# Where the rows of the MLP's operands start in SBUF: multiples of 128 bytes, or steps of 16 bytes and places off a 16-byte line

## The chip, the core and the metric

The kernel runs on one core of a Trainium2 chip. The metric is the device time of one execution in microseconds (us). The time before is the median of three runs. One further execution was recorded by the hardware profiler; the rows that are shown below come from it.

The engines are called as in the profile: PE is TensorE's matrix multiplication, PEld its loading of weights, DVE is VectorE, ACT is ScalarE, POOL is GpSimd and SP is SyncE, which here only issues DMAs. SBUF is the memory on the chip. It has 128 partitions, and a tile lies at the same byte address in all of them, so "where a row starts" is one number.

## The reference

A decoder block on 16 learned tokens and 256 input tokens, with a model width of 2048. A mixer of two attention branches comes first, then a squared-ReLU MLP of width 8192, then a norm. All of it is float32.

```python
for l in range(DEPTH):      # DEPTH = 1
    h = h + hybrid_mixer(rmsnorm(h, norm_mix_g[l]), w_in[l], ...)
    h = h + squared_relu_mlp(rmsnorm(h, norm_mlp_g[l]), w_ff1[l], w_ff2[l])
return rmsnorm(h, final_norm_g)[:, N_META:]

def squared_relu_mlp(xn, w1, w2):
    return jnp.square(jax.nn.relu(xn @ w1)) @ w2
```

`w1` is 2048 x 8192 and `w2` is 8192 x 2048.

## The kernel before

Everything is held transposed: 128 channels lie on the partitions, tokens along the row. 2048 channels are 16 blocks, called k.

Each float32 factor is cut in two, a high part in the type float32r and the remainder, and a product is made of the terms that matter. An operand tile has one row for each k. The row has 2 x 256 columns, the high parts of the 256 tokens and then the low parts. `mac2` (lines 135 to 137) makes two matmuls for each k: a wide one, the high part of the weights (`whi`) on all 512 columns, and a narrow one, the low part (`wlo`) on the first 256. `gemm2` runs them over 16 k into one PSUM bank, so one product of 128 output channels is 32 matmuls. The weights of the next matmul are loaded into TensorE while the present one streams its columns.

Weights come in chunks of 128 x 2048 in the order of `stream()`. SyncE issues two DMAs of 512 KB for each chunk into `raw` (five buffers). ScalarE casts `raw` to `whi` (line 120), and VectorE subtracts to get `wlo` (line 121). Both have five buffers of 4096 bytes a partition, with one k every 512 bytes.

The order of the instructions is worked out by a planner, which simulates the program on a timeline; it may move instructions of one product a little among those of the next.

The MLP runs in four quarters (`for g in range(NG)`, lines 885 to 903). A quarter makes 16 products of `x2` with the first matrix (line 889), and `relu2` turns each into one row of `a` (total, maximum and norm, square, and `split_to`, lines 877 to 882). Then it makes 16 products of `a` with the second matrix, which are added to the residual `h` (line 898). `x2` is written before, a row at a time, as the mixer's last products end (lines 864 to 867). In the last quarter the last four products are made in another order: the low weights on the high part (L912), and then the kept high weights `whi_last` on half of the tokens at a time, 2 x 128 columns (L928).

Operand tiles come from the helper `operand()` (line 218). `og` and `x2` stand one after the other in the slot "s2", which `whi_last` takes over at the end; `x`, `y` and the four `a` stand in the slot "s1". `of` stands in the pool "late". In all of them a row is 2 x 256 columns with 32 columns left out behind it, so rows are 544 columns, 2176 bytes, apart, and the first starts 16 columns, 64 bytes, from the tile's place (for `of` 48 columns from it):

```python
row = 2 * NT + 32
t = pool.tile([P, at + nk * row], F32R, name=nm(name), **kw)
t = t[:, at:].rearrange("p (k r) -> p k r", r=row)
return t[:, :, 16 : 16 + 2 * NT].rearrange("p k (o t) -> p k o t", t=NT)
```

In the allocation of this program, every `whi` and `wlo` buffer starts at 128 modulo 512 bytes, the slots s1 and s2 start at 64, and `whi_last`, which begins with its slot, starts at 64 too.

Of the kernel before, what the change touches and what calls it, by code (L numbers as in the profile page):

```python
# [8 lines left out]
F32R = mybir.dt.float32r  # L9
# [7 lines left out]
P = 128  # L17
D = 2048
KT = D // P
NM = 16  # L20
NT = 256
NA = NM + NT
EPS = 1e-6
FOX_H, FOX_D = 8, 128
# [41 lines left out]
def trunk(ctx: ExitStack, tc: tile.TileContext, hT, w_small, w_all, consts, w_alpha2, out):  # L66
# [3 lines left out]
    def nm(s):  # L70
        serial[0] += 1
        return f"{s}_{serial[0]}"

    const = ctx.enter_context(tc.tile_pool(name="const", bufs=1))
    keep = ctx.enter_context(tc.tile_pool(name="keep", bufs=1))
# [49 lines left out]
    def next_weights(keep_hi=None):  # L125
        c = chunk[0]
        chunk[0] += 1
        parts = []
        for i in range(2):
            hi, lo, step = weight_half(c, i, None if keep_hi is None else keep_hi[:, HK * i : HK * (i + 1), :])  # L130
            step(0, HK)
            parts.append((hi, lo))
        return lambda k: (parts[k // HK][0][:, k % HK, :], parts[k // HK][1][:, k % HK, :])
# [5 lines left out]
    def gemm2(w, x, k0=0, nk=KT):  # L139

        ps = bank(pg, "ps")
        for k in range(nk):
            hi, lo = w(k0 + k)
            mac2(ps, hi, lo, x[:, k], k == 0, k == nk - 1)
        issued()
        return ps
# [18 lines left out]
    def total(ps, t=None):  # L165

        b = tmp.tile([P, NT], F32, tag="evb", name=nm("evb"))
        nc.scalar.copy(b, ps[:, NT:512])  # L168
        if t is None:
            t = tmp.tile([P, NT], F32, tag="evt", name=nm("evt"), bufs=4)  # L170
        nc.vector.tensor_tensor(t, ps[:, 0:NT], b, op=ALU.add)  # L171
        return t
# [42 lines left out]
            nc.vector.scalar_tensor_tensor(r, r, -0.5, v, op0=ALU.mult, op1=ALU.mult)  # L215
            nc.vector.scalar_tensor_tensor(y, r, 1.5, y, op0=ALU.add, op1=ALU.mult)

    def operand(pool, name, nk=KT, at=0, **kw):


        row = 2 * NT + 32
        t = pool.tile([P, at + nk * row], F32R, name=nm(name), **kw)
        t = t[:, at:].rearrange("p (k r) -> p k r", r=row)
        return t[:, :, 16 : 16 + 2 * NT].rearrange("p k (o t) -> p k o t", t=NT)


    h = keep.tile([P, KT, NA + 3], F32, name="h")
# [26 lines left out]
    def gain(i, k):  # L254
        return h[:, k, NA + i : NA + i + 1]
# [60 lines left out]
    for s in range(KT // 2):  # L316
# [5 lines left out]
        for kk in range(2):  # L322
            k = 2 * s + kk
# [15 lines left out]
        at = [(w[0][:, c], w[1][:, c]) for w, n in ((wa, 4), (wb, 3)) for c in range(n)]  # L339
# [118 lines left out]
    def og_tile():  # L458
        if not og_box:
            og_box.append(operand(keep, "og", tag="s2"))  # L460
        return og_box[0]
# [220 lines left out]
    cum.close()  # L682
    branches = ExitStack()
    late = branches.enter_context(tc.tile_pool(name="late", bufs=1, reuse_waits="tile"))
    of = operand(late, "of", FOX_H, 32)
    negc = late.tile([P, FOX_H, NA], F32, name="negc")
    nc.gpsimd.dma_start(negc.rearrange("p h t -> p (h t)"), fdram.to_broadcast([P, FOX_H * NA]))
    fox = ExitStack()
# [137 lines left out]
    for j0 in range(0, KT, 2):  # L826
        gates = ahead if j0 == 0 else [gate() for _ in range(4)]
        w = next_weights()
        for j in range(2):
            t = total(gemm2(w, of, k0=8 * j, nk=8))  # L830
            nc.vector.tensor_tensor(gates[2 * j], gates[2 * j], t, op=ALU.mult)
        for j in range(2):
            t = total(gemm2(next_weights(), og))
            nc.vector.tensor_tensor(t, gates[2 * j + 1], t, op=ALU.mult)
            nc.vector.tensor_tensor(yf[:, j0 + j, :], gates[2 * j], t, op=ALU.add)
    y = operand(keep, "y", tag="s1")
    for j in range(KT):
        split_to(y[:, j, 0, :], y[:, j, 1, :], yf[:, j, :])
# [4 lines left out]


    ht = h[:, :, NM:NA]
    x2 = operand(keep, "x2", tag="s2")

    def square_sum(j, acc):
        if j == 0:
            nc.scalar.activation(acc, ht[:, j, :], AF.Square)  # L850
        else:
            sq = gat.tile([P, NT], F32, tag="hsq", name=nm("hsq"))
            nc.scalar.activation(sq, ht[:, j, :], AF.Square)  # L853
            nc.gpsimd.tensor_tensor(acc, acc, sq, op=ALU.add)  # L854

    def add_residual(j, ps):
        b = tmp.tile([P, NT], F32, tag="evb", name=nm("evb"))
        nc.scalar.copy(b, ps[:, NT:512])
        nc.vector.tensor_tensor(ht[:, j, :], ps[:, 0:NT], ht[:, j, :], op=ALU.add)
        nc.vector.tensor_tensor(ht[:, j, :], ht[:, j, :], b, op=ALU.add)  # L860
# [16 lines left out]
    def relu2(a, f, ps):  # L877
        t = total(ps)
        nc.vector.scalar_tensor_tensor(t, t, 0.0, r2b, op0=ALU.max, op1=ALU.mult)
        s = gat.tile([P, NT], F32, tag="asq", name=nm("asq"))  # L880
        nc.vector.tensor_tensor(s, t, t, op=ALU.mult)
        split_to(a[:, f, 0, :], a[:, f, 1, :], s)

    acc = gat.tile([P, NT], F32, tag="acc", name="acc3", bufs=1)
    for g in range(NG):
        a = operand(keep, "a", tag="s1")
        held = []
        for f in range(KT):
            ps = gemm2(next_weights(), x2)
            if g == 0 and f == 0:  # L890
                held.append(ps)
                continue
            if g == 0 and f == 1:
                relu2(a, 0, held.pop())
            relu2(a, f, ps)
        last = g == NG - 1
        for j in range(KT - NL if last else KT):
            add_residual(j, gemm2(next_weights(), a))
            if last:
                square_sum(j, acc)  # L900
                nc.scalar.activation(ht[:, j, :], ht[:, j, :], AF.Identity, scale=gain(2, j))
                if j == 0:
                    tc.keep_in_program_order(nc.scalar.preload_act_table_set("natural_log_exp_and_others"))
# [155 lines left out]
```

## Time and profile before

| | us |
|---|---|
| median of 3 runs | 1597.07 (1596.95 to 1597.44) |
| span of the profiled execution | 1595.0 |
| PE busy in it | 1585.0 |
| DVE busy | 1060.4 |
| ACT busy | 790.8 |

The profiled execution's own time is its span of 1595.0 us and 2.07 us less than the median of the runs.

How to read the profile's rows. A group of instructions has its line, engine and operation, the tile that is written and those that are read, the shape, the count, then the busy time in us and the mean in ns of one, then the idle time of its engine before it. The duration of a matmul runs on through the pipeline after the last column is in, so matmuls in a stream overlap: the time from one start to the next is less than the duration. Differences between durations of one form can be compared. In the chain in order of time a piece has its start, its length, and how many instructions it merges. Slices are fortieths of the span, in tenths.

### The profile page before, as it was taken

What the parts mean: (1) busy time and instruction counts of PE and PEld (TensorE: products, weight loads), DVE (VectorE), ACT (ScalarE), POOL (GpSimd) and SP (SyncE); (2) the same over time, 40 slices, a digit from 0 to 9 for tenths busy, and PEclk for the clock granted to TensorE, in tenths of its full rate; (3) what the DMA queues carried; (4) which work ended last, traced back from release to release, by engine and by line L of the source; (5) the groups of instructions that cost most, each with busy time, mean ns of one, the idle gap of its engine ahead of it and who ended that gap; (6) DMA issues with size and microseconds to landing.
All of it is one profiled execution on the core that took longest, in us unless ns stands there. A gap on an engine that the chain in (4) does not pass through costs nothing.

```text
span 1595.0 us, 25427 instructions
## 1 busy us (share of the span) xinstructions
PE 1585.0 (99%) x9812; PEld 1428.8 (90%) x9812; DVE 1060.4 (66%) x1659; ACT 790.8 (50%) x1271; POOL 125.2 (8%) x213
## 2 busy tenths in 40 slices
PE   9999999999999999999999999999999999999997
PEld 8999999999998888888888888888888888888887
DVE  7897757676655555555777776567655776567655
ACT  6665444454455444444555544444444444444563
POOL 6011000011100000000011000000000000000022
PEclk9999999999999999999999999999999999999999
DMA  9444545454445555555555555555555555555552
GB/s 323 156 164 155 180 157 183 167 188 164 159 167 181 191 186 189 189 191 187 186 195 186 188 193 187 188 191 190 187 190 190 186 189 193 186 188 193 186 183 97
DMA packets 86602, 293.09 MB, mean 184 GB/s; under 512 B 9112, under 2 KB 16800, under 8 KB 86352
## 3 DMA queue, kind: packets, MB, share of 16 engines
q1 hardware_dynamic: 85872, 289.62, 53.8%
q8 instruction: 77, 1.26, 0.3%
q0 software_dynamic: 176, 1.12, 0.2%
q10 hardware_dynamic: 432, 0.72, 0.1%
q14 instruction: 45, 0.37, 0.1%
HBM read 289.32 MB, written 2.11 MB: 183 GB/s over the span
## 4 chain that ended last, share of the span: by engine, by line
PE 99%; DMA 0%; issue 0%; POOL 0%; ACT 0%; DVE 0%; SPq 0%; POOLq 0%; ACTq 0%
PE ps L136 51%; PE ps L137 27%; PE psa L155 5%; PE psa L154 5%; PE psa L153 5%; PE ps L345 1%; PE ps L350 1%; PE ps L928 1%; PE pa L548 1%; PE ps L912 0%; DMA raw<-w_all_dram 0%; PE po L611 0%; POOL o L976 0%; PE po L188 0%; PE ps L348 0%
## 5 line engine op out<-in xcount | busy, mean ns | idle before, releaser
L121 DVE TENSOR_TENSOR wlo<-raw,whi 128x1024 fp32r<-128x1024 f32 x522 | 641.0, 1228 | 452.8 <-ACT whi L120 449.4
L120 ACT CAST whi<-raw 128x1024 fp32r<-128x1024 f32 x522 | 548.1, 1050 | 660.0 <-PE ps L136 493.1
L136 PE MATMUL ps<-x,whi 128*128 128x512 f32 x1952 | 683.8, 393 | 0.0
L137 PE MATMUL ps<-x,wlo 128*128 128x256 f32 x1952 | 548.5, 281 | 0.0
L136 PEld LDWEIGHTS ps<-x,whi 128*128 128x128 f32 x1952 | 366.1, 188 | 80.4
L137 PEld LDWEIGHTS ps<-x,wlo 128*128 128x128 f32 x1952 | 368.3, 189 | 0.1
L136 PE MATMUL ps<-a,whi 128*128 128x512 f32 x960 | 334.3, 392 | 0.0
L137 PE MATMUL ps<-a,wlo 128*128 128x256 f32 x960 | 269.1, 281 | 0.0
L136 PEld LDWEIGHTS ps<-a,whi 128*128 128x128 f32 x960 | 179.8, 188 | 39.9
L137 PEld LDWEIGHTS ps<-a,wlo 128*128 128x128 f32 x960 | 181.1, 189 | 0.3
L153 PE MATMUL psa<-x,whi 128*128 128x272 f32 x624 | 181.2, 290 | 0.0
L155 PE MATMUL psa<-x,whi 128*128 128x272 f32 x624 | 181.1, 290 | 0.0
L154 PE MATMUL psa<-x,wlo 128*128 128x272 f32 x624 | 179.4, 288 | 0.0
L153 PEld LDWEIGHTS psa<-x,whi 128*128 128x128 f32 x624 | 118.1, 189 | 0.4
L154 PEld LDWEIGHTS psa<-x,wlo 128*128 128x128 f32 x624 | 117.4, 188 | 0.0
L155 PEld LDWEIGHTS psa<-x,whi 128*128 128x128 f32 x624 | 117.2, 188 | 0.0
L136 PE MATMUL ps<-og,whi 128*128 128x512 f32 x256 | 89.6, 392 | 0.0
L136 PE MATMUL ps<-y,whi 128*128 128x512 f32 x256 | 89.1, 392 | 0.0
L854 POOL TENSOR_TENSOR acc<-acc,hsq 128x256 f32<-128x256 f32 x26 | 28.5, 1097 | 769.2 <-ACT hsq L853 769.2
L137 PE MATMUL ps<-og,wlo 128*128 128x256 f32 x256 | 71.9, 281 | 0.0
L137 PE MATMUL ps<-y,wlo 128*128 128x256 f32 x256 | 71.8, 281 | 0.0
L171 DVE TENSOR_TENSOR evt<-ps,evb 128x256 f32<-128x256 f32 x158 | 65.9, 418 | 0.5 <-ACT evb L168 0.5
(301 smaller groups left out, 1437.0 us busy)
## 6 DMA issues: line engine op xcount, KB each, us to landing
raw<-w_all_dram SPq DMA_DIRECT2D x537, 512.0 KB, 3.6
raw<-w_all_dram SPq DMA_DIRECT2D x8, 384.0 KB, 6.6
h<-hT_dram SPq DMA_DIRECT2D x8, 275.0 KB, 6.7
negc<-fdram POOLq DMA_DIRECT2D x1, 1088.0 KB, 8.0
out_dram<-o SPq DMA_DIRECT2D x2, 512.0 KB, 2.7
raw<-w_all_dram SPq DMA_DIRECT2D x2, 256.0 KB, 3.9
room<-w_small_dram SPq DMA_DIRECT2D x1, 320.0 KB, 7.4
out_dram<-o ACTq DMA_DIRECT2D x1, 320.0 KB, 3.1
```

Of the source, the lines that this page charges most:

```text
L120: nc.scalar.copy(hi[:, k, :], r)
L121: nc.vector.tensor_tensor(lo[:, k, :], r, hi[:, k, :].bitcast(F32), op=ALU.subtract)
L136: nc.tensor.matmul(ps, hi, x, start=first, stop=False)
L137: nc.tensor.matmul(ps[:, 0:NT], lo, x[:, 0, :], start=False, stop=last)
L153: nc.tensor.matmul(ps[:, 0:NA], hi, x_hi[:, k], start=(k == 0), stop=False)
L154: nc.tensor.matmul(ps[:, 0:NA], lo, x_hi[:, k], start=False, stop=(k == KT - 1))
L155: nc.tensor.matmul(ps[:, X_LO], hi, x_lo[:, k], start=False, stop=(k == KT - 1), skip_group_check=True)
L171: nc.vector.tensor_tensor(t, ps[:, 0:NT], b, op=ALU.add)
L345: nc.tensor.matmul(ps, hi, x[:, k], start=st, stop=False)
L350: nc.tensor.matmul(ps[:, 0:NT], lo, x[:, k, 0], start=False, stop=sp)
L548: nc.tensor.matmul(dst, k[:, a], q[:, a, :], start=(a == 0), stop=(a == 1))
L854: nc.gpsimd.tensor_tensor(acc, acc, sq, op=ALU.add)
```

## The change

`operand()` gets the place of the first row (`at`, in columns of 4 bytes) and the distance between rows (`row`) as arguments. With the defaults the rows stand as before, at 16 columns and 544 apart; a tile is now never larger than its rows. `of` uses the defaults, so its tile is 32 columns shorter and its first row is 16 columns from the tile's place.

`x2` has its rows from column 16, 516 columns (2064 bytes) apart. The first two `a` have theirs from column 80, also 516 apart. The third `a` starts at column 18 and the fourth at column 17, with 520 columns (2080 bytes) between rows. In bytes modulo 16 the rows of `x2` and of the first two `a` start at 0, those of the third at 8 and those of the fourth at 4. What is computed is the same, and so are the instructions and their number.

```diff
-    def operand(pool, name, nk=KT, at=0, **kw):
-
-
-        row = 2 * NT + 32
-        t = pool.tile([P, at + nk * row], F32R, name=nm(name), **kw)
-        t = t[:, at:].rearrange("p (k r) -> p k r", r=row)
-        return t[:, :, 16 : 16 + 2 * NT].rearrange("p k (o t) -> p k o t", t=NT)
+    def operand(pool, name, nk=KT, at=16, row=2 * NT + 32, **kw):
+
+        t = pool.tile([P, nk * (2 * NT + 32)], F32R, name=nm(name), **kw)
+        if at + nk * row > nk * (2 * NT + 32):
+            return t.rearrange("p (k r) -> p k r", r=row)[:, :, at : at + 2 * NT].rearrange("p k (o t) -> p k o t", t=NT)
+        t = t[:, at : at + nk * row].rearrange("p (k r) -> p k r", r=row)
+        return t[:, :, 0 : 2 * NT].rearrange("p k (o t) -> p k o t", t=NT)
...
-    of = operand(late, "of", FOX_H, 32)
+    of = operand(late, "of", FOX_H)
...
-    x2 = operand(keep, "x2", tag="s2")
+    x2 = operand(keep, "x2", at=16, row=2 * NT + 4, tag="s2")
...
-        a = operand(keep, "a", tag="s1")
+        a = operand(keep, "a", at=(80, 80, 18, 17)[g], row=2 * NT + (4, 4, 8, 8)[g], tag="s1")
```

## The prediction

> **What bounds the kernel now.** I read the page's shares, slices and chain first, then the stretch of the MLP, then the single matmuls in it.
>
> ```profile
> span 1595.0 us, 25427 instructions
> PE 1585.0 (99%) x9812; PEld 1428.8 (90%) x9812; DVE 1060.4 (66%) x1659; ACT 790.8 (50%) x1271; POOL 125.2 (8%) x213
> PEclk9999999999999999999999999999999999999999
> PE 99%; DMA 0%; issue 0%; POOL 0%; ACT 0%; DVE 0%; SPq 0%; POOLq 0%; ACTq 0%
> PE ps L136 51%; PE ps L137 27%; PE psa L155 5%; PE psa L154 5%; PE psa L153 5%; PE ps L345 1%; PE ps L350 1%; PE ps L928 1%; PE pa L548 1%; PE ps L912 0%; DMA raw<-w_all_dram 0%; PE po L611 0%; POOL o L976 0%; PE po L188 0%; PE ps L348 0%
> ```
>
> TensorE is the chain: 99% of it, at full granted clock in every slice, and 78% in the two lines of `mac2`. The executions had a median of 1597.07 us; this profiled one spans 1595.0, so 2.07 us lie around the span, and I add them to every sum.
>
> Next the MLP, cut at the borders between its halves (first matrix, second matrix, in turn). The columns are the stretch, its length, and the busy time and count of TensorE.
>
> ```profile
> 1049.76:1138.94 89.18, 89.18 (x514) 1.00 0.56 189
> 1138.94:1228.11 89.17, 89.17 (x513) 1.00 0.55 189
> 1228.11:1317.28 89.17, 89.17 (x513) 1.00 0.56 189
> 1317.28:1406.46 89.18, 89.18 (x514) 1.00 0.56 190
> ```
>
> Two stretches read `x2`, two read `a`, and all take the same 89.17 us without a gap. A half has 16 products of 16 pairs, so a wide and a narrow matmul together cost 89.17 / 256 = 0.348 us. In such a stretch nothing but the rate at which TensorE streams columns sets the time. The change touches where these columns lie, so it acts on the bound itself, with no cover over it in either direction.
>
> The matmuls by form, in the stretch that reads the third `a`:
>
> ```profile
> L136 PE MATMUL ps<-a,whi 128*128 128x512 f32 x253 | 88.1, 392 | 0.0
> L137 PE MATMUL ps<-a,wlo 128*128 128x256 f32 x252 | 70.6, 281 | 0.0
> L137 PEld LDWEIGHTS ps<-a,wlo 128*128 128x128 f32 x253 | 47.7, 189 | 0.1
> L136 PEld LDWEIGHTS ps<-a,whi 128*128 128x128 f32 x253 | 47.4, 188 | 10.5
> ```
>
> 256 more columns take 392 - 281 = 111 ns more, which is 0.434 ns a column. 16 bytes are four columns, 1.7 ns. That is my price for one more piece of 16 bytes, if TensorE fetches in such pieces.
>
> **The change part by part.** No instruction is added or taken away. What moves is the first byte of every row that a matmul streams. By the allocation of this program, each weight tile starts at 128 modulo 512 and its k steps are 512 bytes, so `whi[k]` and `wlo[k]` are always at 128. Both slots, s1 and s2, start at 64. Before, row k stands at 64 + 64 + 2176k, which is 128k from the weights' place modulo 512. After, `x2` stands at 16k, the first two `a` at 256 + 16k, the third at 8 + 32k and the last at 4 + 32k.
>
> Matmuls affected: `x2` 4 x 16 products x 32 = 2048; the first two `a` 1024; the third 512; the last 12 x 32, and 64 of L912 and 128 of L928, 576. In all 4160. The bound of 0.2%, about what a measurement of this kernel can tell from no change, is 3.2 us, or 0.77 ns for each of them. So the whole question is about fractions of a percent of a matmul.
>
> Term A, the place beside the weights. The trace shows two sets of places on the same tile `a`, both of 256 columns, in the tail where no weight is being cast: L912 against `wlo`, at multiples of 128 from the weights, and L928 against `whi_last`, whose slot starts at 64, so at odd multiples of 64.
>
> ```profile
> 1562.51 5.68 PE ps L912 x48
> ...
> 1571.96 7.47 PE ps L928 x64
> ```
>
> From the chain in order of time: 5.68 / 48 = 118.3 ns against 7.47 / 64 = 116.7 ns each. The place matters, by 1.6 ns. How much one and the same line varies as k goes through the four places it has now is in the answer for L136:
>
> ```profile
> L136 PE MATMUL ps<-a,whi x238: 388/393/397, 1317.1 to 1399.7; 128*128 128x512 f32 x119
> L136 PE MATMUL ps<-x,whi x7: 390/392/393, 1314.7 to 1316.8; 128*128 128x512 f32 x7
> ```
>
> Minimum, median and maximum: a spread of 3 to 9 ns around 392, on `x2` as on `a`. One more row shows starts that are not multiples of 64. In the GLA outputs `a0h` and its weights start 32 bytes past one, in the FoX outputs `pah` and its weights do not, with the same 256 columns:
>
> ```profile
> L190 PE MATMUL po<-a0h,v0l x16: 278/280/281, 99.3 to 302.2; 128*128 128x256 f32 x16
> L190 PE MATMUL pof<-pah,val x8: 278/278/280, 352.6 to 485.9; 128*128 128x256 f32 x8
> ```
>
> The median is 2 ns higher. So term A lies between -1.6 ns (all new places like L928's) and +2 ns (all like `a0h`'s): -6.7 to +8.3 us over 4160. A sweep in steps of 16 or 32 bytes spreads the rows evenly over half of the 512 bytes or all of them, good and bad places alike. Only a quarter of the swept places are multiples of 64, of which the rows say anything good. I take a quarter of -1.6, that is -0.4 ns: -1.7 us. [...]
>
> Term B, rows off a 16-byte line. In the last two quarters a row of 512 columns begins and ends inside a 16-byte piece, and touches 129 of them in place of 128. At 1.7 ns each for 512 + 576 = 1088 matmuls this is +1.9 us. [...] Its upper end is the rate of plain float32, the slowest streaming that the trace has:
>
> ```profile
> L548 PE MATMUL pa<-qx,kx 128*128 128x208 f32 x16 | 3.8, 359 | 0.0
> L548 PE MATMUL pa<-qx,kx 128*128 128x80 f32 x16 | 2.3, 264 | 0.0
> ```
>
> (359 - 264) / 128 = 0.742 ns a column, 0.308 above the 0.434 of the MLP's form. The last `a` is streamed over 192 x 768 + 192 x 256 = 196,608 columns, so at that rate it costs +61 us. I take +1.9: the stream is contiguous in all quarters, and only its two ends change. [...]
>
> Term C, what other engines do with the rows. ScalarE and VectorE write them, and VectorE reads one half back, at the new places:
>
> ```profile
> L121 DVE TENSOR_TENSOR wlo<-raw,whi 128x1024 fp32r<-128x1024 f32 x522 | 641.0, 1228 | 452.8 <-ACT whi L120 449.4
> L879 DVE SCALAR_TENSOR_TENSOR evt<-evt,r2b 128x256 f32<-128x256 f32 x64 | 27.0, 425 | 2.0
> L881 DVE TENSOR_TENSOR asq<-evt 128x256 f32<-128x256 f32 x64 | 27.0, 424 | 2.0
> L176 DVE TENSOR_TENSOR a<-asq,a 128x256 fp32r<-128x256 f32 x64 | 26.6, 419 | 0.0
> L171 DVE TENSOR_TENSOR evt<-ps,evb 128x256 f32<-128x256 f32 x158 | 65.9, 418 | 0.5 <-ACT evb L168 0.5
> L175 ACT CAST a<-asq 128x256 fp32r<-128x256 f32 x64 | 25.5, 401 | 0.0
> ```
>
> A product of the first matrix lasts 89.17 / 16 = 5.57 us. VectorE does 2 x 1.23 + 0.42 + 0.42 + 0.42 + 0.42 = 4.14 us in it. If the write of L176 took twice its 0.42, it would be 4.56, still under 5.57. The product that runs meanwhile hides it, so it costs 0. Without that cover the doubling would be 0.42 us for each of 64 rows, 27 us. What would be late then is the last row, `a[15]`, for the first product of the second matrix. The reuse of slots s1 and s2 adds no wait: a row is first written after a whole product on another operand, 5.57 us after the last reader of the old tile.
>
> Term D, `of`. Its tile is 128 bytes shorter, and row 0 stands 128 bytes lower. With a row step of 2176 the places are still all multiples of 128, the same set in another order of k. The tiles behind it in the late pools move by 128 bytes, and their starts modulo 64 stay. Cost 0, with at most the 2 ns of L190 on 2 calls x 3 matmuls x 8 heads, 0.1 us.
>
> The sum: 1595.0 - 1.7 + 1.9 + 2.07 = 1597.3 us.
>
> **The rivals.**
>
> Slower, by a fetch of 32 bytes. If TensorE takes rows in aligned pieces of 32 bytes, every row that does not start on one needs a further piece, 8 columns, 3.5 ns. These are half of `x2` (1024), half of the first two `a` (512) and all of the last two (1088), 2624 matmuls: +9.2 us, 1606.3. For it: no matmul of this kernel's MLP starts at an odd multiple of 16 now, so nothing excludes it. Against it: pieces of 64 bytes would cost 7 ns at `a0h`, and L190 shows 2. It decides from 1.2 ns a matmul.
>
> Much slower, by rows 4 bytes off. If a column pair that straddles a line needs two accesses, the last quarter streams near the rate of L548: +61 us, 1658. For it: the MLP's form is the fastest stream that the kernel has, so it has least to spare. Against it: nothing more than that the rows are contiguous.
>
> Faster, by better places. If multiples of 128 bytes are the worst meeting of moving rows and weights, and all other places are like L928's, the 4160 matmuls gain 1.6 ns each and the ragged ends are hidden: -6.7 us, 1590.4. For it: 118.3 against 116.7 ns. Against it: the 2 ns that `a0h` loses at a place that is no multiple of 128. It decides from 0.77 ns a matmul.
>
> The change cannot fail to take place: the rows lie where the program puts them.
>
> **How the numbers follow.** The forecast, no change that can be measured, gets 0.40, since its two terms are of one size and of opposite sign. The fetch of 32 bytes, or another cost of a few ns on ragged rows, gets 0.26, and the straddling pairs 0.11: two ways to be slower, neither excluded by any row. Better places get 0.23. So faster 0.23, same 0.40, slower 0.37. The forecast's own range is 1594 to 1600. The range of 8 in 10 reaches down to 1590, the end of term A. Upward it goes to the fetch of 32 bytes with part of term A's upper end, 1612. Left out are the straddling pairs (0.11) and some 0.06 in the tails.
>
> **What would show it.** In the profile after, each half on `x2` or on the first two `a` should take 89.17 - 512 x 0.0004 = 89.0 us, and the half on the third `a` 89.17 + 512 x 0.0013 = 89.8. If the halves on `x2` are longer than before, term A has the wrong sign. If the third and the last differ by over 1%, the bytes inside a line matter. If L136's maximum is far over 393, single rows stall. I would be wrong above all if the stream has a unit that the aligned rows of now never showed.

## The result: slower by 0.6%, nearly all of it inside the MLP

The changed kernel takes 1606.36 us (median; 1605.82 to 1606.71) against 1597.03 before (the median of four executions; 1597.07 was that of the first three). The ratio is 1.0058, with a 95% interval of 1.0046 to 1.0071. The forecast was no change that can be measured, 1597.3 us. The time lies in the range of 1590 to 1612, on the side that had 0.37, and outside the forecast's own range of 1594 to 1600.

The order of the instructions is the same on every engine. First the page of the changed kernel, its span, shares and chain by engine:

```profile
span 1605.0 us, 25427 instructions
PE 1595.2 (99%) x9812; PEld 1432.2 (89%) x9812; DVE 1059.9 (66%) x1659; ACT 790.8 (49%) x1271; POOL 124.9 (8%) x213
PE 99%; issue 0%; POOL 0%; DMA 0%; ACT 0%; POOLq 0%; DVE 0%; ACTq 0%
```

TensorE is busy 10.2 us longer, and its share of the chain is what it was. No wait has come in; the matmuls themselves are longer. The halves of the MLP, one on `x2`, one on the second `a`, one more on `x2`, the one on the third `a`, and then the twelve whole products on the fourth `a` (columns as in the prediction's windows):

```profile
1052.06:1142.19 90.13, 90.13 (x513) 1.00 0.58 187
1142.19:1232.31 90.12, 90.12 (x513) 1.00 0.59 187
1232.31:1322.44 90.13, 90.13 (x513) 1.00 0.59 187
1322.44:1413.00 90.56, 90.56 (x514) 1.00 0.58 187
1503.14:1571.55 68.41, 68.41 (x387) 1.00 0.58 186
```

Before, each half took 89.17, so twelve products took 66.88. The four halves on `x2` and the two on the first two `a`, all on 16-byte lines (a line is here no more than the 16 bytes from one multiple of 16 to the next), lose 0.96 us each, 5.8 together. The half on the third `a`, 8 bytes off a line, loses 1.39, and the twelve products on the fourth, 4 bytes off, 1.53. The tail reads the fourth `a` as well; in the chain in order of time:

```profile
1571.55 5.88 PE ps L912 x48
...
1581.32 7.84 PE ps L928 x64
```

That is 122.5 ns for each matmul of both lines, where it was 118.3 and 116.7: 64 x 4.2 + 128 x 5.8 = 1.0 us. The sum is 9.7 us. The two profiled spans differ by 10.0, of which 0.4 came ahead of the MLP (its first matmul starts at 871.42 us in place of 871.02); the medians differ by 9.3.

### The profile page after: what moved, and what is told of

Read it like the earlier page. It is cut to its first block, busy times and chain, and to the rows that moved or that the text cites. A ratio compares the mean times of both kernels' runs of the same rounds, so it can differ in the third digit from the quotient of the medians.

```text
span 1605.0 us, 25427 instructions
## 1 busy us (share of the span) xinstructions
PE 1595.2 (99%) x9812; PEld 1432.2 (89%) x9812; DVE 1059.9 (66%) x1659; ACT 790.8 (49%) x1271; POOL 124.9 (8%) x213
## 4 chain that ended last, share of the span: by engine, by line
PE 99%; issue 0%; POOL 0%; DMA 0%; ACT 0%; POOLq 0%; DVE 0%; ACTq 0%
PE ps L136 51%; PE ps L137 26%; PE psa L155 5%; PE psa L154 5%; PE psa L153 5%; PE ps L345 1%; PE ps L928 1%; PE ps L350 1%; PE pa L548 1%; PE ps L912 0%; PE po L611 0%; POOL o L976 0%; DMA h<-hT_dram 0%; PE po L188 0%; PE ps L348 0%
## 5 line engine op out<-in xcount | busy, mean ns | idle before, releaser
L136 PE MATMUL ps<-x,whi 128*128 128x512 f32 x1952 | 687.6, 395 | 0.0
L136 PEld LDWEIGHTS ps<-x,whi 128*128 128x128 f32 x1952 | 366.3, 188 | 83.9
L136 PE MATMUL ps<-a,whi 128*128 128x512 f32 x960 | 339.1, 396 | 0.0
L136 PEld LDWEIGHTS ps<-a,whi 128*128 128x128 f32 x960 | 180.6, 188 | 43.0
L136 PE MATMUL ps<-og,whi 128*128 128x512 f32 x256 | 89.5, 392 | 0.0
L136 PE MATMUL ps<-y,whi 128*128 128x512 f32 x256 | 89.1, 392 | 0.0
```

The lines of the kernel that those rows point to most:

```text
L136: nc.tensor.matmul(ps, hi, x, start=first, stop=False)
```

## Experiments

Three theories stood at the start. By the theory of the fetch in 32 bytes (a rival of the prediction, 1606.3 us) every row that does not start on a multiple of 32 costs 3.5 ns more. By the theory of the place alone, a row costs what its place relative to the weights costs, whatever stands before it. By the theory of the step, the distance between rows decides. Since all eight halves of the MLP are measured apart, one kernel can hold five layouts. Places and steps are in bytes from the weights' place, modulo 512, as in the prediction: rows 2176 bytes apart have a step of 128, rows 2048 bytes apart a step of 0. Where no ratio is given, the kernel ran once, and parts of its one trace are compared.

### Same step as before, other starts

```diff
-    x2 = operand(keep, "x2", at=16, row=2 * NT + 4, tag="s2")
+    x2 = operand(keep, "x2", at=20, row=2 * NT + 32, tag="s2")
...
-        a = operand(keep, "a", at=(80, 80, 18, 17)[g], row=2 * NT + (4, 4, 8, 8)[g], tag="s1")
+        a = operand(keep, "a", at=(24, 32, 18, 17)[g], row=2 * NT + (32, 32, 32, 32)[g], tag="s1")
```

> Rows 2176 bytes apart as before, but started off the multiples of 128: x2 at 16 + 128k from the weights' place, the four a at 32, 64, 8 and 4 + 128k. Half by half (89.17 us each before; 90.12 on x2 and on the first two a after, 90.55 on the third a after). Theory of the fetch in pieces of 32 bytes: x2 91.0, first a 89.2, second a 89.2, third a 91.0, total about +10 us. Theory of the place alone (a pair takes what the row at that place took in the trace after, period 256): x2 89.9, first a 89.5, second a 90.1, and the third and fourth more. Theory of the step (steps of 128 keep the meeting of rows and weights as it was, wherever they start): all halves on 16-byte lines within 0.2 of 89.2, and only the third and fourth a, off a line, longer, by 0.3 to 1.4.

1603.15 us. The windows of this kernel, in the order `x2` (16 off), first `a` (32), second (64), third (8):

```profile
1050.76:1140.34 89.58, 89.58 (x514) 1.00 0.58 188
961.17:1050.76 89.59, 89.59 (x515) 1.00 0.57 189
1140.34:1229.96 89.62, 89.62 (x515) 1.00 0.58 187
1319.56:1409.68 90.12, 90.12 (x515) 1.00 0.57 188
```

Rows that all start at odd multiples of 16 cost the same as rows on 32 and on 64. The fetch in 32 bytes said 91.0 against 89.2, so it falls, although the time that it gave for the change, 1606.3, is the time that was measured. The step alone does not decide either: at the same step, 0 took 89.17 and 16, 32 and 64 take 0.4 more. The row 8 bytes off costs 0.5 beyond those.

### Other steps

The lines that replace the same two of the changed kernel:

```diff
+    x2 = operand(keep, "x2", at=16, row=2 * NT + 8, tag="s2")
...
+        a = operand(keep, "a", at=(20, 16, 18, 17)[g], row=2 * NT + (8, 16, 4, 4)[g], tag="s1")
```

> Other steps: x2 at 32k from the weights' place (all even multiples of 16), first a at 16 + 32k (all odd multiples), second a at 64k, third at 8 + 16k and fourth at 4 + 16k. Theory of the fetch in pieces of 32 bytes: x2 89.2, first a 91.0, second a 89.2, third a 91.0. Theory of the place alone: x2 90.1, first a 90.1, second a 90.4. Theory of the step: x2 and first a alike, and the second a, with the larger step, nearer to 89.2 than both.

1603.94 us. `x2` on all even multiples of 16, first `a` on all odd ones, second `a` on multiples of 64, third 8 off a line at steps of 16:

```profile
1050.53:1140.33 89.80, 89.80 (x515) 1.00 0.58 188
961.12:1050.53 89.41, 89.41 (x515) 1.00 0.58 188
1140.33:1229.73 89.40, 89.40 (x515) 1.00 0.57 188
1319.54:1410.17 90.63, 90.63 (x514) 1.00 0.57 186
```

The odd multiples are the faster ones here. By the place alone, 89.41, 89.80 and 89.40 should have been 90.1, 90.1 and 90.4, so that theory falls too: one place does not have one price. By the step, `x2` and the first `a` should have been alike; they differ by 0.39.

### One place for all rows, and the weights moved instead of the rows

The same two lines again:

```diff
+    x2 = operand(keep, "x2", at=16, row=2 * NT + 0, tag="s2")
...
+        a = operand(keep, "a", at=(48, 32, 20, 64)[g], row=2 * NT + (0, 0, 0, 0)[g], tag="s1")
```

> Rows 2048 bytes apart, so that all rows of a tile stand at one place from the weights: x2 at 0, the four a at 128, 64, 16 and 192. Theory of the place alone: halves of 89.3 (x2), 92.2 (128), 88.8 (64), 89.9 (16), and the rate of the last a that of 91.4 (192). Theory of the fetch in pieces of 32 bytes: 89.2 for x2 and the first, second and fourth a, 91.0 for the third. Theory of the step: no half need follow the row of its place in the trace after; what a row costs depends on the rows before it.

The second kernel has this ahead of the weights' buffers besides:

```diff
+    gap = wp.tile([P, 16], F32, name="gap", bufs=1)
```

> As e_const, with a tile of 64 bytes put in ahead of the weights' buffers, so that the weights move by 64 bytes and the rows do not. If the place relative to the weights decides, the halves change places with e_const (period 256): the first a takes what e_const's second a took (64), the second a what e_const's x2 took (0), x2 what e_const's last a took (192), and the last a what e_const's first a took (128). If the rows' own address decides, each half is as in e_const within 0.1.

1603.37 and 1606.26 us. In the second kernel the products before the MLP meet moved weights too, so the halves are compared and not the totals. First the kernel without the gap: `x2` (0), first `a` (128), second (64), third (16):

```profile
1052.00:1142.46 90.46, 90.46 (x515) 1.00 0.58 187
962.13:1052.00 89.87, 89.87 (x515) 1.00 0.58 188
1142.46:1232.90 90.44, 90.44 (x515) 1.00 0.58 187
1321.65:1410.40 88.75, 88.75 (x514) 1.00 0.59 190
```

And with it, the same tiles in the same order, whose places are now 448, 64, 0 and 464:

```profile
1054.26:1144.69 90.43, 90.43 (x514) 1.00 0.57 186
964.83:1054.26 89.43, 89.43 (x515) 1.00 0.58 189
1144.69:1233.60 88.91, 88.91 (x514) 1.00 0.58 190
1324.04:1413.66 89.62, 89.62 (x515) 1.00 0.57 188
```

Three of the four halves shown moved though their rows did not, by 0.44 to 1.53 us. The half on `y`, ahead of the MLP, has its rows in both kernels where the kernel before has them. First without the gap, then with it:

```profile
782.61:871.78 89.17, 89.17 (x514) 1.00 0.59 191
784.70:874.32 89.62, 89.62 (x514) 1.00 0.59 190
```

Without the gap it takes 89.17 or 89.18 in every trace that leaves `y` there, the kernel before among them. With the gap its rows stand at 64 + 128k, and 89.62 is what the second `a` took at these places in the first experiment. So the rows' own address cannot be all, and where the weights stand has its part.

Of the four exchanges that the place relative to the weights foretold, the last `a`, now at 128, took the 89.87 of the first `a` there. `x2`, now at 448, took the 90.43 that the last `a` took at 192 (256 of its pairs at 353.3 ns), but it had taken 90.46 without the gap, so this one decides nothing. The two others did not come: place 0 took 90.46 in one kernel and 88.91 in the other, and place 64 took 90.44 and 89.43. Rows 2048 bytes apart at place 16 took 88.75, less than any layout so far; the fetch in 32 bytes had 91.0 for them. The prices of the theory of the place alone (89.3, 92.2, 88.8 and 89.9 in the order of the first four lines) are all missed by over 1 us.

One place has two rates even within the kernel without the gap. These are its first product on `x2`, the fourth of the same half, and the third half on `x2`:

```profile
871.78:877.33 5.55, 5.55 (x34) 1.00 0.61 190
888.64:894.29 5.65, 5.65 (x34) 1.00 0.58 190
1232.90:1321.65 88.75, 88.75 (x515) 1.00 0.59 189
```

Rows and weights stand alike in all of them. In the first half the pairs take 346 to 347 ns (5.55 us for 16) until the two matmuls of the norm (L207 and L208) come between, and from then on 349, 350 and 361 in turn (5.65 us for 16). The second and the fourth half on `x2` have the slow rate, 90.46 and 90.45; the third has the fast one. So what ran before counts, and 90.46 against 88.91 at place 0 may be these two rates, with no part in it of the moved weights.

### Blocks of pairs, measured by themselves

The kernel before, with this behind its last output; `flat` is the weights of `whi_last`, and each call is one block of pairs, whose results are not used:

```diff
+    rows = keep.tile([P, KT * 2 * NA], F32R, tag="s1", name="rows")
...
+    def block(name, place, step, shift=0, m=P, wide=True, narrow=True, wstep=P, reps=2):
...
+                row = rows[:, at + k * step // 4 : at + k * step // 4 + 512]
+                for on, c, n in ((wide, 0, 512), (narrow, 2048, 256)):
+                    if on:
+                        jobs.append((c + k * wstep + shift, row[:, 0:n], n))
+        for i, (c, r, n) in enumerate(jobs):
+            pin(nc.tensor.matmul(ps[0:m, 0:n], flat[:, c : c + m], r, start=(i == 0), stop=(i == len(jobs) - 1)))
```

> The kernel before, and behind its last output some 40 separate blocks of pairs (one wide and one narrow matmul, as in mac2) on a tile of constant rows, each block with its own place, step of rows, shift of the weights or width of the weights; so its total is some 450 us longer and only the blocks are read. Before, a pair takes 348.3 ns; on steps of 16 bytes 352.0. Theory of the meeting (rows meet the load of the next weights, and the place relative to the weights decides): moving rows and weights together by 64 or 128 bytes changes a pair by under 0.3 ns, and with weights of only 64 or 32 columns a pair gets shorter and the steps of 16 and of 128 bytes come within 1 ns of each other. Theory of the rows' own address: moving the weights alone changes nothing, and with narrow weights the difference of 3.7 ns between the two steps stays. Theory of the ragged ends (a 129th piece of 16 bytes): rows at 4, 8 and 12 bytes off a line cost the same, some 1.7 ns a matmul more than at 16, in the wide and the narrow alike. Theory of column pairs that straddle (units of 8 bytes): 8 costs what 16 does, 4 and 12 cost alike and more, and more in the wide than in the narrow.

From its chain in order of time, a block a line: start, length, name, matmuls. A block is 32 pairs. `stb` and `stf` have steps of 16 and 128 from place 0; `pla` and `plb` have rows 2048 bytes apart at places 0 and 16; `ofa` to `ofd` have steps of 128 with starts at 16, 8, 4 and 12; `ma`, `mb` and `mc` have weights of 64 columns, with steps of 128, of 16, and of 128 from 4.

```profile
1629.38 11.28 PE stb L1018 x64
...
1674.28 11.16 PE stf L1018 x64
...
1693.84 11.30 PE pla L1018 x64
1705.14 11.10 PE plb L1018 x64
...
1940.12 11.19 PE ofa L1018 x64
1951.31 11.40 PE ofb L1018 x64
1962.71 11.47 PE ofc L1018 x64
1974.17 11.10 PE ofd L1018 x64
...
2007.89 11.15 PE ma L1018 x64
2019.04 11.11 PE mb L1018 x64
2030.15 11.52 PE mc L1018 x64
```

The blocks give back what the kernels did: 11.28 / 32 = 352.5 ns a pair at steps of 16 (the halves on `x2` after: 90.13 / 256 = 352.1), 348.8 at steps of 128 (348.3 before, without the block's first matmul). So the loss needs no other engine: from 1599.58 us, the first block, to 2097.76 the chain holds matmuls alone, and no weights are cast in that time.

With weights of 64 columns the two steps come together, 11.15 and 11.11. The next kernel repeats it: 11.14 and 11.10 with 64 columns, 11.15 and 11.26 with 128. So on 16-byte lines the loss of the small step hangs on the width of the weights. Narrower weights are loaded and also make a narrower result, and the blocks do not separate the two. The pair at steps of 128 did not get shorter by it, which the theory of the meeting had wrong. The row 4 bytes off stays expensive with narrow weights (11.52), so that part, 11.52 against 11.15, is the rows' own. It is a price of each matmul and not of each column: by themselves, 32 wide matmuls took 7.36 us on a line and 7.47 at 4 off, 32 narrow ones 3.79 and 3.88, which is 3.4 and 2.8 ns for each.

Rows and weights moved together, the other test of the theory of the meeting, bear it out in part. By 64 bytes a block went from 11.16 to 11.14 and another stayed at 11.31; by 128 bytes one went from 11.10 to 11.09, but two others from 11.31 to 11.16 and from 11.30 to 11.10. So the place of the rows relative to the weights does not fix the rate by itself either.

The starts inside a line are no matter of straddling units of 8 bytes, since 8 off (`ofb`, 11.40) costs nearly what 4 off does (`ofc`, 11.47). Nor is it the 129th piece, since 12 off, which has one as well (`ofd`, 11.10), is the cheapest of the four. These are single blocks. The next kernel takes averages, and asks for the state left by the block before.

```diff
+    block("loa", 0, 2176)
+    block("lob", 16, 2176)
...
+    block("hye", 128, 2048)
+    block("hyf", 0, 2048)
```

> The kernel before with 65 blocks of pairs behind it, as in p1_blocks; only the blocks are read. What a start off a 16-byte line costs, averaged over eight places (steps of 2176 bytes from 0, 16 to 112) and not at one. Theory of the ragged ends: 4, 8 and 12 bytes off alike, some 3.4 ns a pair over 0. Theory of straddling column pairs: 8 bytes off costs nothing, 4 and 12 alike and more. Third theory, from p1_blocks, where 4 off took 358.2, 8 off 356.6, 12 off 346.7 and 16 349.6 ns a pair: the cost grows the lower the start is in its line, 12 off costs nothing on average, 8 some 4 and 4 some 9 ns. With weights of 64 columns, theory of the meeting: the four places that took 353.2 to 353.5 or less by turns with rows 2048 bytes apart (0, 64, 112, 192, against 346.6 at 16 and 144) come together within 2 ns of each other; if the meeting with the weights' load plays no part they stay 6.7 ns apart. Blocks at place 0 behind blocks at 16, 144 and 128: if a place has one price, 353.2 each time; if the state left by the block before counts, some of them 346.7.

Eight blocks each at steps of 128, from places 0, 16 to 112, and then the same with 4, 8 and 12 bytes added:

```profile
1619.90:1709.56 89.66, 89.66 (x514) 1.00 0.00 1
1709.56:1800.72 91.16, 91.16 (x513) 1.00 0.00 1
1800.72:1891.15 90.43, 90.43 (x514) 1.00 0.00 1
1891.15:1980.20 89.05, 89.05 (x513) 1.00 0.00 1
```

A window has 256 pairs: 350.2 ns on a line, 356.1 for 4 bytes off, 353.2 for 8, and 347.9 for 12. So 4 off costs 5.9 a pair, 8 off 3.0, and 12 off wins 2.3, as the third theory of this expectation had it in order, with a smaller price for 4. Single blocks scatter, in us:

```
off   from 0    16     32     48     64     80     96    112
 0   11.15  11.19  11.19  11.20  11.21  11.41  11.22  11.09
 4   11.35  11.30  11.31  11.31  11.46  11.46  11.47  11.51
 8   11.26  11.31  11.21  11.30  11.39  11.33  11.31  11.31
12   11.20  11.04  11.31  11.14  11.10  11.15  11.04  11.09
```

The best, 12 off from 16 (place 28), is 11.04, 345.0 ns a pair. Single blocks at other steps have the same order: at steps of 32, from two places, 11.23 and 11.19 on a line, 11.39 and 11.37 at 4, 11.31 and 11.30 at 8, 11.11 and 11.12 at 12; at steps of 16 it is 11.26, 11.41, 11.30 and 11.09. With rows 2048 bytes apart 4 and 8 off both took 11.31 in the first kernel, where place 0 took 11.30, so there they cost nothing over that.

Last, from the same chain, two blocks with weights of 64 columns and rows 2048 bytes apart, at places 0 and 16, and three blocks at place 0 behind others:

```profile
2115.29 10.88 PE nma L1018 x64
...
2159.24 11.30 PE nme L1018 x64
...
2282.01 11.31 PE hyb L1018 x64
...
2304.41 11.10 PE hyd L1018 x64
...
2326.73 11.30 PE hyf L1018 x64
```

With narrow weights, place 0 fell from 11.30 to 10.88 and place 16 rose from 11.10 to 11.30. They did not come together, as the theory of the meeting wanted. 10.88 is less than any block with 128 columns took (11.04 at least), so the width of the weights has its part, in a way that I cannot give as a formula. 11.30 is a rate that wide weights show too, at place 0, so place 16 may only have come into another of its rates. And one layout at place 0 took 11.31, 11.10 and 11.30 behind other blocks. These three blocks wrote different PSUM banks, but the halves on `x2` above, each of which goes through the same banks, had two rates as well. So a place has at least two rates, and which one a stretch settles in depends on its past. A theory that gives each place one price cannot hold.

### The two ragged quarters put on a line

```diff
-        a = operand(keep, "a", at=(80, 80, 18, 17)[g], row=2 * NT + (4, 4, 8, 8)[g], tag="s1")
+        a = operand(keep, "a", at=(80, 80, 20, 20)[g], row=2 * NT + (4, 4, 8, 8)[g], tag="s1")
```

> The changed kernel with its third and fourth a moved to column 20, 520 columns apart: steps of 32 bytes from place 16, all on 16-byte lines. d_step32 had 89.41 us for a half of this layout. If the bytes inside a line are what made these two quarters longer: third half 89.4 in place of 90.55, last quarter's pairs 349 in place of 356 ns, L912 and L928 near 118 in place of 122: together -3.3 us, about 1603.1. If the steps of 32 bytes made them longer: no change, 1606.4.

1603.13 us, ratio to the kernel before 1.0038 (1.0025 to 1.0052). The third `a`'s half, and the twelve products on the fourth:

```profile
1322.32:1411.73 89.41, 89.41 (x513) 1.00 0.58 189
1501.86:1568.92 67.06, 67.06 (x386) 1.00 0.58 188
```

The same step of 32 bytes, on a line: 89.41 in place of 90.56, 67.06 in place of 68.41. So 3.2 us of the 9.3 are the bytes inside a line, and 6.1 are the steps on lines.

### Two layouts that are faster than before

```diff
-    x2 = operand(keep, "x2", at=16, row=2 * NT + 4, tag="s2")
+    x2 = operand(keep, "x2", at=20, row=2 * NT, tag="s2")
```

and the same for `og`, `y` and the four `a`, with `of` at column 52.

> All operand tiles (og, of, y, x2 and the four a) with rows 2048 bytes apart at place 16, which took 88.75 us a half in e_const and 346.67 ns a pair in p1_blocks, against 89.17 and 348.3 before. If that place keeps its price wherever it is used: 2000 pairs of the MLP and 640 of og, of and y gain 1.6 ns each, -4.2 us, about 1592.8. If the state left by the product before decides which of several rates a tile settles in: between 1592.8 and 1602.

1592.72 us, ratio 0.9973 (0.9963 to 0.9983): place 16 keeps its price, 88.75 us a half.

The other layout is the kernel before with rows 12 bytes off a line, at place 28:

```diff
-        return t[:, :, 16 : 16 + 2 * NT].rearrange("p k (o t) -> p k o t", t=NT)
+        return t[:, :, 23 : 23 + 2 * NT].rearrange("p k (o t) -> p k o t", t=NT)
...
-    of = operand(late, "of", FOX_H, 32)
+    of = operand(late, "of", FOX_H)
```

> The kernel before with one number changed: all operand rows start 7 columns (28 bytes) later, 12 bytes off a 16-byte line, at 28 + 128k from the weights' place. In p2_blocks this layout took 344.96 ns a pair against 348.28 at 128k. If a start 12 bytes off a line costs nothing and this layout keeps its rate in the kernel: halves of 88.31 us in place of 89.17, 2000 pairs of the MLP and 640 of og, of and y gain 3.3 ns, -8.8 us, about 1588.2. If every start off a line costs, as my term B has it: +1.7 ns on each of their matmuls, +9 us, 1606. If the state left by the work before decides: anything between 1588 and 1603.

and the rows of `x` besides:

```diff
-    x_row = keep.tile([P, KT, 2 * NA], F32R, tag="s1", name="x")
+    x_row = keep.tile([P, KT * 2 * NA + 32], F32R, tag="s1", name="x")
+    x_row = x_row[:, 7 : 7 + KT * 2 * NA].rearrange("p (k r) -> p k r", r=2 * NA)
```

> As best28, and the rows of x too start 28 bytes later: 928 further pairs gain 3.3 ns, -3.1 us against best28. The 1872 matmuls of 272 columns on x come to stand at 92 and 28 in place of 64 and 0 modulo 128; by the rates of those places in p2_blocks (348.25 and 344.96 against 350.00 and 348.28 a pair) they gain another 1 ns each, -1.5 us: about 1583.6. If the 272-column matmuls lose instead, between 1585 and 1590.

1588.84 us, ratio 0.9948 (0.9934 to 0.9961), and 1583.52 us, ratio 0.9916 (0.9903 to 0.9930). A half on `x2` and one on `a`, in the first of the two kernels:

```profile
1046.59:1134.91 88.32, 88.32 (x513) 1.00 0.58 191
1134.91:1223.24 88.33, 88.33 (x513) 1.00 0.59 191
```

88.32 in place of 89.17, as 256 x 344.96 ns had it. So an unaligned start is no loss by itself.

## Why the prediction was right or wrong

**The bound.** Right: in the MLP the rate at which TensorE streams is the time, and every ns of a matmul came through: TensorE is busy 10.2 us longer, and the span is 10.0 longer. Term C was right as well. The writes did not get longer; in the changed kernel:

```profile
L176 DVE TENSOR_TENSOR a<-asq,a 128x256 fp32r<-128x256 f32 x64 | 26.6, 419 | 0.0
L175 ACT CAST a<-asq 128x256 fp32r<-128x256 f32 x64 | 25.5, 401 | 0.0
```

Term D was too small to be seen. No single row stalls by much: L136's maximum went from 397 ns to 405 on the third `a` and 410 on the fourth, and the median went with it, from 393 to 395 and 399.

**Term A is the step that failed.** I took -0.4 ns a matmul and had the bounds at -1.6 and +2. On 16-byte lines the change costs 0.96 us a half, 0.96 / 512 = +1.9 ns a matmul, near the upper bound, and with the two ragged quarters on a line it costs 6.1 us where I had -1.7. The failure was to read L928's 116.7 ns against L912's 118.3 as good and bad places. The two lines differ in the shape of their rows as well, 2 x 128 columns against 256, and the order turns with the layout: in the first kernel with place 28 it is 7.57 / 64 = 118.3 ns for L928 and 5.60 / 48 = 116.7 for L912. The places before were not the bad ones: among the layouts on 16-byte lines measured inside the kernel, 89.17 is a low one (88.75 to 90.46). The sweeps over places on 16-byte lines that were measured all lose (89.40 to 90.13). The row of `a0h`, 2 ns higher, pointed that way, and I gave it no weight. The sum had a slip besides: a quarter of the places are multiples of 64 only for `x2` and the first two `a`, 3072 matmuls, so that term A would have been -1.2 us and not -1.7.

**Term B was too small, and for the wrong reason.** I had +1.9 us from one further piece of 16 bytes; no run shows that TensorE takes rows in such pieces, and the term was an estimate. The two quarters cost 3.2 us beyond their steps: (90.56 - 89.41) / 512 = 2.2 ns a matmul for 8 off, (68.41 - 67.06) / 384 = 3.5 ns for 4 off. A further piece is not the cause, since 12 off has it too and is faster than 0 in the blocks (347.9 ns a pair against 350.2) and in two kernels (1588.84 and 1583.52 us against 1597.16).

**The rivals.** The fetch of 32 bytes gave 1606.3 and the measurement 1606.36. It is wrong all the same: 89.58 and 89.59 for rows at 16 and at 32, 89.41 for odd multiples of 16 against 89.80 for even ones. A right total from the wrong mechanism is a coincidence here, of a loss spread over all rows with one that was to fall on some five in eight of them. The range reached up to 1612 for this rival's sake and for term A's upper end, so it is in part luck that the time lies inside it. The straddling pairs at the rate of plain float32 are excluded: 4 off loses 2% in the pairs and 4% in L912, not 70%. Better places do exist, but the change did not go to them.

**The width of the weights.** A change of the weights' width alone moved a block at place 0 from 11.30 to 10.88 us, by 4%, and by 2% against the 11.10 that the same place took at its faster rate. Whether this comes from the load of the weights or from the narrower result is not shown: the blocks do not separate the two.

**What stays open.** Why a start 12 bytes into a line is the fast one, what the rates of a place are, and what decides which of them a stretch settles in. The runs show that the place of the weights, their width and the past of the stretch all count; they do not show the mechanism.

## What to carry to other kernels

Where TensorE streams float32r without a gap, the start of the rows was worth 0.6% one way (1606.36 us against 1597.03) and 0.8% the other (1583.52 against 1597.16) here, with no instruction changed, and neither "aligned" nor "a spread over all places" is the good choice by itself. Measure candidate layouts in blocks behind the kernel, on its own shapes and weights, dozens in one run; for the two layouts carried over, places 16 and 28, the rates found so came back in the kernel to within a microsecond in 1600. Repeat each block behind different ones, since one layout had two rates here (11.10 and 11.31 us). And when a total agrees with a rival, still test what the rival says of the single rows.

## What the runs showed that I had not expected

Starting the rows 12 bytes off a 16-byte line, over eight places, took 347.9 ns a pair against 350.2 on a line, and in the whole kernel 1588.84 and 1583.52 us against 1597.2. Two blocks with the same instructions on the same rows and weights took 11.10 and 11.31 us, and one tile in one kernel took 90.46 and 88.75 us a half, by what ran before them. And the four starts in a line are ordered 12, 0, 8, 4 by time (347.9, 350.2, 353.2 and 356.1 ns a pair), with steps of some 3 ns between neighbours.
